# Batch normalisation of 32x256x128x128: the first tile's left half loaded in four pieces, the parameters in eight rows, 544 more columns for VectorE

## The chip, the cores and the metric

The kernel runs on one core of one Trainium2 chip. The metric is device time in microseconds (us). Before the change it is 2482.19 us, the median of three runs (2502.58, 2481.61 and 2482.19). One more execution was taken with the hardware profiler; every duration below comes from that one.

## The reference

```python
mean = running_mean.reshape(1, -1, 1, 1)
var = running_var.reshape(1, -1, 1, 1)
return gamma * (x - mean) / np.sqrt(var + 1e-5) + beta
```

All arrays are float32. `x` is 32x256x128x128 (536.9 MB) and so is the output; the four parameters have 256 values each. Per channel the computation is one multiply and one add, `x*scale + shift`, with `scale = gamma/sqrt(var + eps)` and `shift = beta - mean*scale`. Everything that is read is read once, and everything that is written is written once.

## The kernel before

**Tiles.** 256 channels are two blocks of 128, so `x` is cut into 64 tiles (`NT`) of 128 partitions x 16384 float32 (8.39 MB, 64 KB in each partition). Three buffers `bufs[0..2]` (`NBUF`) hold a tile each; a tile is loaded into a buffer, changed in place and stored from it.

**Loads.** SyncE (SP) issues all loads on its hardware queue. Tile 0 comes in two halves of 128x8192: the left half (line 89, semaphore `early`), then, behind the four parameter loads, the right half (line 96, semaphore `first[0]`). Tiles 1 and 2 follow whole (line 98). Tile i from 3 on (line 161) waits until the store of tile i-3 has freed its buffer (`stored`).

**Parameters.** Line 92 loads each of the four parameters as `NE` = 16 equal rows of 256 values (1 KB a row) into `rows`, a 32x1024 array that VectorE (DVE) has zeroed before (line 90; the first parameter load waits for that). When all four have landed (`fetched`), DVE transposes 32x32 blocks (line 109), copies four columns into place (line 113), and DVE and ScalarE (ACT) compute `scale_t` and `shift_t` (lines 115 to 125). The transpose reads row 0 of each block only, so one row would do for the values.

**Arithmetic.** Tile 0 is shared: DVE does columns 0 to 8191 as soon as the left half has landed (line 154, a wait for `early` at 16), then the columns up to `VHEAD` (line 155, after the right half); ACT does columns `VHEAD` to 16383. The last tile is shared in the same way at `VLAST` = 9216. All other tiles are ACT's alone (line 142 is the helper's activation, line 131 the helper's tensor_scalar).

**Stores.** GpSimd (POOL) issues the stores of tiles 0 to 60 through its software queue (line 173), each after ACT's part (`adone`), that of tile 0 also after DVE's two parts (`vdone`). ACT issues the last three itself. The order of work on every engine is written out by hand.

A DMA transfer's semaphore is raised by 16 in all when it has landed, so a wait at 16 is a wait for a whole transfer.

Of the kernel before, what the change touches and what calls it, by code (L numbers as in the profile page):

```python
# [9 lines left out]
PAD = 936  # L10
NHEAD = 3
NTAIL = 3
VHEAD = 8336
VLAST = 9216


@with_exitstack
def kernel(
# [9 lines left out]
    nc = tc.nc  # L28
# [4 lines left out]
    P = nc.NUM_PARTITIONS  # L33
    assert C % P == 0
    NCB = C // P
    HW = H * W
    NT = N * NCB
    B = 32
    NQ = P // B
    NE = 16  # L40
    NPAR = 4

    xr = x.rearrange("n (cb p) h w -> (n cb) p (h w)", p=P)
# [5 lines left out]
    bufs = [data.tile([P, HW], f32, name=f"t{s}", tag=f"t{s}") for s in range(NBUF)]  # L49
# [15 lines left out]
    early = tc.alloc_semaphore("early")  # L65
# [7 lines left out]
    with tc.tile_critical():  # L73
        count = [0]

        def step(inst, sem=None, value=None):
            if sem is not None:
                inst._wait_ge(sem, value)
            elif count[0]:
                inst._wait_ge(vec, count[0])  # L80
            inst.then_inc(vec, 1)
            count[0] += 1
            return count[0]

        left, right = slice(0, HW // 2), slice(HW // 2, HW)
        last = NT - 1


        nc.sync.dma_start(out=bufs[0][:, left], in_=xr[0][:, left]).then_inc(early, 16)
        zeroed = step(nc.vector.memset(rows[:], 0.0))  # L90
        for r, ap in enumerate((running_var, gamma, beta, running_mean)):
            inst = nc.sync.dma_start(out=rows[0:NE, r * C : (r + 1) * C], in_=ap.partition_broadcast(NE))  # L92
            if r == 0:
# [6 lines left out]
        def landed(i):  # L100
            if i < NHEAD:
                return first[i], 16
            s = i % NBUF
            before = 1 if s < NHEAD else 0
            return loaded[s], 16 * (i // NBUF + 1 - before)
# [6 lines left out]
        for q in range(NQ):  # L112
# [3 lines left out]
            out=std_t[:],  # L116
            in_=var_t,
# [11 lines left out]
        def vector_part(i, first_col, end):  # L129
            t, cb = bufs[i % NBUF], i % NCB  # L130
            return nc.vector.tensor_scalar(  # L131
                out=t[:, first_col:end],
                in0=t[:, first_col:end],
                scalar1=scale_t[:, cb : cb + 1],
                scalar2=shift_t[:, cb : cb + 1],
                op0=mybir.AluOpType.mult,
                op1=mybir.AluOpType.add,
            ).then_inc(vdone, 1)
# [12 lines left out]
        def share(i):  # L151
            return VHEAD if i == 0 else VLAST if i == last else 0

        vector_part(0, 0, HW // 2)._wait_ge(early, 16)
        vector_part(0, HW // 2, VHEAD)._wait_ge(first[0], 16)
        vector_part(last, 0, VLAST)._wait_ge(*landed(last))

# [57 lines left out]
```

## Time and profile before

| what | us |
|---|---|
| median of three runs | 2482.19 |
| profiled execution, its own time | 2482.56 |
| its span, first to last instruction | 2480.8 |
| first load issued (line 89) | 0.96 |
| left half landed, after its issue | 12.7 |
| right half landed, after its issue at 3.93 | 19.6 |
| first store issued (line 173) | 30.93 |
| last load landed, ACT starts the last tile | 2450.06 |
| last store issued by ACT | 2456.45 |

| engine | busy us | share of the span |
|---|---|---|
| DVE | 13.5 | 1% |
| ACT | 885.5 | 36% |
| POOL | 32.7 | 1% |

The profile's page gives the busy time of each engine, the share of the 16 DMA engines that were moving data in 40 equal slices of the span, the DMA queues (q1 is SP's hardware queue, q10 is ACT's, q0 is POOL's software queue) and the chain of waits that ended last. TensorE does nothing. The trace also holds each DMA packet with its start, duration, queue and size, and the time of each semaphore update by a DMA; it does not say which of the 16 engines carried a packet. A packet of a load or store is one partition's row.

### The profile page before, as it was taken

Reading aid. Unit: us, or ns where it says so; the run is one execution under the profiler, and the core shown is the slowest. Engines: PE = TensorE matmul, PEld = TensorE weight load, DVE = VectorE, ACT = ScalarE, POOL = GpSimd, SP = SyncE. Lnnn points to the kernel's source line nnn. Section 1 sums busy time; section 2 is a strip of 40 time slices with the busy share of each in tenths; the row PEclk is TensorE's granted clock in tenths of the full one; section 3 lists DMA queues with packets and bytes.
Section 4 is the critical chain, followed back from the end, with each engine's and each line's share of the span. In section 5 each row is a group of like instructions: output and inputs, shape, how many; then the busy total and the mean of one; then the engine's idle time right before and its main releaser. Section 6 shows DMA issues by size and latency. Waiting matters only on the chain.

```text
span 2480.8 us, 277 instructions
## 1 busy us (share of the span) xinstructions
DVE 13.5 (1%) x14; ACT 885.5 (36%) x66; POOL 32.7 (1%) x65
## 2 busy tenths in 40 slices
DVE  1000000000000000000000000000000000000000
ACT  2342433424324243242342423424334243342432
POOL 0000000000000000000000000000000000000000
DMA  9999999999999999999999999999999999999999
GB/s 413 433 431 431 440 435 427 440 439 424 440 439 424 440 439 424 440 439 428 435 439 431 432 440 434 428 440 435 427 440 437 425 440 439 424 440 439 426 437 406
DMA packets 18707, 1073.84 MB, mean 433 GB/s; under 512 B 2128, under 2 KB 2192, under 8 KB 2192
## 3 DMA queue, kind: packets, MB, share of 16 engines
q1 hardware_dynamic: 9488, 536.94, 50.0%
q0 software_dynamic: 8784, 511.71, 47.6%
q10 hardware_dynamic: 432, 25.17, 2.3%
q14 instruction: 3, 0.02, 0.0%
HBM read 536.94 MB, written 536.87 MB: 433 GB/s over the span
## 4 chain that ended last, share of the span: by engine, by line
another core or an unknown queue 61%; ACT 35%; DMA 2%; issue 0%; SPq 0%; DVE 0%; ACTq 0%; DVEq 0%
ACT t L142 35%; DMA t<-in_x_dram 2%; SPq L92 0%; DVE rows L90 0%; ACTq L173 0%; SPq L96 0%; DVE eps_t L108 0%; DVEq L210 0%; SPq L73 0%
## 5 line engine op out<-in xcount | busy, mean ns | idle before, releaser
L142 ACT ACTIVATE t<-t,shift_t,scale_t 128x16384 f32<-128x16384 f32 (+1 forms) x64 | 883.9, 13811 | 1555.8 <-DMA t<-in_x_dram 1555.8
L173 POOL DMA_DIRECT2D out_dram<-t x61 | 32.5, 533 | 2315.8 <-ACT t L142 2315.8
L131 DVE TENSOR_SCALAR t<-t,scale_t,shift_t 128x8192 f32<-128x8192 f32 (+2 forms) x3 | 10.0, 3326 | 2427.6 <-DMA t<-in_x_dram 2427.5
L115 ACT ACTIVATE std_t<-par,eps_t 128x2 f32<-128x2 f32 x1 | 0.3, 295 | 14.3 <-DVE par L113 14.3
L115 ACT ACT_TABLE_LOAD x1 | 1.3, 1283 | 0.9 <-SPq L73 0.9
L109 DVE STREAM_TRANSPOSE turned<-rows 32x1024 f32<-32x1024 f32 x1 | 1.2, 1232 | 12.1 <-DMA rows<-in_running_mean_dram 12.1
L90 DVE MEMSET rows<- 32x1024 f32 x1 | 0.9, 912 | 1.2 <-SPq L73 1.2
L113 DVE COPY par<-turned 32x8 f32<-32x8 f32 x4 | 0.6, 162 | 0.1
L122 DVE RECIPROCAL rstd_t<-std_t 128x2 f32<-128x2 f32 x1 | 0.2, 166 | 0.4 <-ACT std_t L115 0.4
L124 DVE TENSOR_TENSOR ms_t<-par,scale_t 128x2 f32<-128x2 f32 x1 | 0.2, 163 | 0.0
L123 DVE TENSOR_TENSOR scale_t<-par,rstd_t 128x2 f32<-128x2 f32 x1 | 0.2, 160 | 0.0
L125 DVE TENSOR_TENSOR shift_t<-par,ms_t 128x2 f32<-128x2 f32 x1 | 0.2, 160 | 0.0
L199 POOL MEMSET const-float32-0.0<- 128x1 f32 x1 | 0.1, 98 | 0.2 <-issue 0.2
L199 POOL MEMSET const-bfloat16-1.0<- 128x1 bf16 x1 | 0.1, 101 | 0.0
L199 POOL MEMSET const-float32-1.0<- 128x1 f32 x1 | 0.1, 98 | 0.0
L199 POOL MEMSET const-uint8-127<- 128x1 uint8 x1 | 0.1, 98 | 0.0
L108 DVE MEMSET eps_t<- 128x1 f32 x1 | 0.1, 59 | 0.1
## 6 DMA issues: line engine op xcount, KB each, us to landing
t<-in_x_dram SPq DMA_DIRECT2D x2, 4096.0 KB, 16.1
t<-in_x_dram SPq DMA_DIRECT2D x63, 56.0
out_dram<-t POOLq DMA_DIRECT2D x61, 45.5
out_dram<-t ACTq DMA_DIRECT2D x3, 32.0
rows<-in_running_var_dram SPq DMA_DIRECT2D x1, 16.0 KB, 11.2
rows<-in_gamma_dram SPq DMA_DIRECT2D x1, 16.0 KB, 11.1
rows<-in_beta_dram SPq DMA_DIRECT2D x1, 16.0 KB, 10.9
rows<-in_running_mean_dram SPq DMA_DIRECT2D x1, 16.0 KB, 10.9
```

The costliest lines, as they stand in the source:

```text
L90: zeroed = step(nc.vector.memset(rows[:], 0.0))
L109: step(nc.vector.transpose(out=turned[:], in_=rows[:]), fetched, 16 * NPAR)
L113: placed = step(nc.vector.tensor_copy(out=flat[q * B : (q + 1) * B], in_=blocks[:, :, q, 0]))
L115: nc.scalar.activation(out=std_t[:], in_=var_t, func=mybir.ActivationFunctionType.Sqrt, bias=eps_t[:], scale=1.0,)._wait_ge(vec, placed).t ...
L122: step(nc.vector.reciprocal(out=rstd_t[:], in_=std_t[:]), act, 1)
L123: step(nc.vector.tensor_mul(out=scale_t[:], in0=gamma_t, in1=rstd_t[:]))
L124: step(nc.vector.tensor_mul(out=ms_t[:], in0=mean_t, in1=scale_t[:]))
L125: ready = step(nc.vector.tensor_sub(out=shift_t[:], in0=beta_t, in1=ms_t[:]))
L131: return nc.vector.tensor_scalar(out=t[:, first_col:end], in0=t[:, first_col:end], scalar1=scale_t[:, cb : cb + 1], scalar2=shift_t[:, cb ...
L142: return nc.scalar.activation(out=t[:, first_col:], in_=t[:, first_col:], func=mybir.ActivationFunctionType.Identity, bias=shift_t[:, cb : ...
L173: eng.dma_start(out=outr[i], in_=bufs[i % NBUF][:], **packet)._wait_ge(adone, i + 1).then_inc(written, 16)
L199: nc = _bacc.Bacc("TRN2", target_bir_lowering=False, num_devices=1)
```

## The change

The left half of tile 0 is no longer one transfer of 128x8192 but four: columns 2304 to 8191 of all partitions, columns 0 to 2303 of partitions 16 to 127, and columns 0 to 2303 of partitions 0 to 7 and of partitions 8 to 15. All four raise `early`, and the first DVE part waits for 64 of it instead of 16. Each parameter is loaded in 8 equal rows instead of 16. `VHEAD` goes from 8336 to 8880, so DVE's second part of tile 0 has 688 columns instead of 144, and ACT's part 7504 instead of 8048.

```diff
-VHEAD = 8336
+VHEAD = 8880
+CUT = 2304
+ODD = 8
...
-    NE = 16
+    NE = 8
...
-        nc.sync.dma_start(out=bufs[0][:, left], in_=xr[0][:, left]).then_inc(early, 16)
+        side, most = slice(0, CUT), slice(CUT, HW // 2)
+        heads = [(slice(0, P), most), (slice(2 * ODD, P), side), (slice(0, ODD), side), (slice(ODD, 2 * ODD), side)]
+        for part, cols in heads:
+            nc.sync.dma_start(out=bufs[0][part, cols], in_=xr[0][part, cols]).then_inc(early, 16)
...
-        vector_part(0, 0, HW // 2)._wait_ge(early, 16)
+        vector_part(0, 0, HW // 2)._wait_ge(early, 16 * len(heads))
```

The order of instructions on DVE, ACT and POOL is the same as before; on SP three transfers are added ahead of the parameter loads.

## The prediction

> **What bounds the kernel.** I read the page first: span, digits of the DMA, queues.
>
> ```profile
> span 2480.8 us, 277 instructions
> ...
> DMA  9999999999999999999999999999999999999999
> ...
> HBM read 536.94 MB, written 536.87 MB: 433 GB/s over the span
> ```
>
> No slice has DMA below 90%, while ACT, the busiest engine, has 36%. So the 16 DMA engines are the bound; the question is whether their rate or their gaps can move. For that, busy times by stage, each row one tile period (the stores of consecutive tiles are issued 38.64 us apart) or a whole number of them; the columns are stretch, length, DVE, ACT, POOL, clock, DMA share, GB/s:
>
> ```profile
> 14.50:53.14 38.64, 7.32 (x11) 7.71 (x3) 0.67 (x1) 1.00 1.02 437
> 53.14:91.78 38.64, 0.00 (x0) 13.96 (x2) 0.53 (x1) 1.00 1.00 434
> 91.78:130.42 38.64, 0.00 (x0) 13.80 (x1) 0.53 (x1) 1.00 1.01 434
> 130.42:169.06 38.64, 0.00 (x0) 14.04 (x1) 0.53 (x1) 1.00 0.98 417
> 169.06:207.70 38.64, 0.00 (x0) 14.04 (x1) 0.53 (x1) 1.00 1.00 434
> ...
> 284.98:1057.78 772.80, 0.00 (x0) 280.79 (x20) 10.63 (x20) 1.00 1.00 434
> ```
>
> From 169 us on the rate stands at 434 GB/s, and 2 x 8.39 MB / 38.64 us is 434.2: 27.1 GB/s for each of the 16. In the packet records a 64 KB row takes 2418 ns, and the next begins 3 ns before its end, load or store alike. All 1073.84 MB at 434.2 GB/s are 2473.1 us. The span is 7.7 us more: **nothing at the head can gain more than 7.7 us, 0.3%**. From the packet records the 7.7 are: 1.97 until the first packet; 0.6 more for the first packets, which take 1.81 us on average and not 1.21; 0.2 for their spread (they start from 1.97 to 2.82, mean 2.18); 0.6 around the parameter packets (an engine's last left packet ends at 12.50 on average, its first right packet at 14.32: 1.82 for a packet of 1.21); 1.5 of packets lengthened while the stores join (19 packets by 9.0 us together at 31 to 36 us, 27 by 4.5 at 91 to 101, 25 by 8.6 at 129 to 138, hardly any after; 23.9 in all over 16 engines); 0.8 by which the slowest engine ends (2478.65) after the mean of all (2477.86); 2.15 from there to the end. That is 7.8.
>
> Now the head, in order of time (start, duration, engine, line):
>
> ```profile
> 0.96 0.37 SPq L89 DMA_DIRECT2D t<-in_x_dram  x1
> ...
> 2.16 0.34 SPq L92 DMA_DIRECT2D rows<-in_running_var_dram  x1
> ...
> 3.93 0.44 SPq L96 DMA_DIRECT2D t<-in_x_dram  x1
> 4.41 1.02 SPq L98 DMA_DIRECT2D t<-in_x_dram  x2
> 14.40 1.23 DVE L109 STREAM_TRANSPOSE turned<-rows 32x1024 f32<-32x1024 f32 x1 [12.14 <-DMA rows<-in_running_mean_dram]
> ...
> 17.64 4.55 DVE L131 TENSOR_SCALAR t<-t,scale_t,shift_t 128x8192 f32<-128x8192 f32 x1
> 23.53 7.09 ACT L142 ACTIVATE t<-t,shift_t,scale_t 128x8048 f32<-128x8048 f32 x1 [6.79 <-DMA t<-in_x_dram]
> 23.53 0.35 DVE L131 TENSOR_SCALAR t<-t,scale_t,shift_t 128x144 f32<-128x144 f32 x1 [1.34 <-DMA t<-in_x_dram]
> 30.93 0.67 POOL L173 DMA_DIRECT2D out_dram<-t  x1 [30.49 <-ACT t L142]
> ```
>
> The reader is to see that everything is issued by 5.43 us while the left half keeps the engines until 12.3: issue has 7 us of cover.
>
> **The change, part by part.**
>
> *SP.* Three more issues of 0.37 to 0.5 us put the last head piece at about 2.6 us. The first parameter load, which waited until 2.16 for the memset, goes at about 2.65; it, the right half and tiles 1 and 2 move back by 0.5 us. Behind 7 us of cover that costs nothing; without cover, the 0.5.
>
> *Left half.* The bytes are the same, the division over engines may not be. In the queue rows of the page the parameter loads show one packet a row (2192 packets under 2 KB less 2128 under 512 B are 64, which is 4 loads of 16 rows), so an eight-row transfer has eight packets and touches eight engines at most; the trace has no such transfer and cannot say which. The 112 rows are seven for each of 16. If both eight-row pieces go to the same eight engines, these get nine rows of 9216 B and the others seven; one row is 9216 B / 27.1 GB/s = 0.34 us, so +0.34 for eight engines and -0.34 for eight. If they go to different eights, zero. The packets of 9216 B that replace part of the 32 KB ones cost between nothing (64 KB and 32 KB packets run at the same rate) and a parameter packet's bubble (0.6 us for four, 0.15 each) for the two odd rows.
>
> *Parameters.* Eight rows are eight packets: at least eight engines lose a transfer's packet, and the 0.6 us around four of them falls to zero there if it is always the same eight; the other eight keep it.
>
> *Sum.* The kernel ends when its slowest engine does. The last store's sixteen updates come at 2477.79 to 2478.37 us and one at 2479.00. With everything on the same eight, the loaded engines shift by +0.34 and the others by -0.34 - 0.6 = -0.94. If the straggler is among the relieved, the end is 2478.37 + 0.34 = 2478.71 at most, -0.3 us; if among the loaded, +0.34; with 0.3 for the two odd packets, +0.6. The trace does not say which; that engine's lag is mostly its lengthened packets (2.1 us, the others 1.2 to 1.6), and those come after the head. The mean over all engines is (0.34 - 0.94)/2 = -0.3, and the bounds' middle is about +0.1. I take **-0.2**, nearer the mean, as the loaded engines' lag is the only thing pushed up.
>
> The Trainium skill (DMA: Bandwidth & Descriptors, section on why a DMA increments its semaphore by 16 and not by 1) says that a transfer uses the largest number of engines up to 16 that divides its outermost dimension, on a hardware queue the lowest-numbered ones. By that all six eight-row transfers fall on the same eight, and the sum is the first case; no row here shows it.
>
> *DVE, ACT.* 544 columns cost DVE 544 x 4.55/8192 = 0.30 us, hidden under ACT's part, which falls by 544 x (7.09 - 6.36)/(8048 - 7168) = 0.45 to 6.64 (6.36 is ACT's row on the last tile's 7168 columns). The first store goes at about 30.5 to 30.9, as the right half may land up to 0.35 later. Parameters up to 0.35 later make DVE's left part end at 22.6, still before 23.5. An earlier store gains nothing: the engines have loads of tiles 1 and 2 to move until 91 us, and total bytes decide.
>
> **The numbers.** The profiled execution took 2482.56, its span and 1.76 around it; the sum gives 2482.36, and the median of the three runs is 0.37 below the profiled one: **2482.0**.
>
> **Rivals.**
>
> 1. *Start-up contention goes* (12%). The two eights would run 1.28 us apart (0.34 + 0.94), half of a 2418 ns packet, when the stores join. Lengthened packets die out once engines are spread, which speaks for it; against, the spread before was already 0.6 us and did not help. Price: a third to all of 1.5 us, 2480.7 to 2481.5.
>
> 2. *The pieces cost a fixed time each, or contention at the head grows* (14%). With one more round of lengthened packets (0.6 us, that of 31 to 36 us) up to double the 1.5, 2482.6 to 2483.5 and above. Against a fixed cost: four parameter loads between two halves cost 0.6 us together. The Trainium skill (DMA: Bandwidth & Descriptors, anatomy of one DMA) fits 2.0 us plus bytes/436 GB/s to one transfer and advises against small ones. By that three more transfers in a row would add 6 us, 2488; four parameter loads in 0.6 us disagree, as the queue overlaps them.
>
> 3. *Contention that does not die out* (8%), the slower side. The shift of phases at the stores' joining could leave a pattern in which packets are lengthened in every tile. Place: the first packets of each load, as at 129 to 138 us. Price: that round's 8.6/16 = 0.54 us x 60 tiles = 32 us, 2514; it exceeds 1% from 0.41 us a tile. For it: the run of 2502.58 is 20 us over the others, 0.33 us a tile, and no profile explains it. Against: every period from 169 us on is at 434.
>
> 4. *The split does nothing* (3%): the odd rows spread evenly, 2482.2.
>
> My forecast, 2481.6 to 2482.7, has the remaining 63%.
>
> **Range and chances.** 2480.6 to 2484.2: rival 1 below; above, +0.6 and double contention (+1.5). It leaves out rival 3 and half of rival 2, 15%. A measurement of this kernel can tell about 1%, 25 us, from no change. Faster by that is excluded by the 7.7 us (1% is kept for what I overlook); slower needs half of rival 3, 4%; within 1%: 95%.
>
> **What would show it.** Right: periods from 169 us on at 434 GB/s; 32 packets between 512 B and 2 KB in place of 64; the left half landing over a spread 0.7 us wider than before; transpose at 14.4 to 14.8; ACT's first part about 6.64; first store near 30.7. Wrong: a period below 430 after 200 us (rival 3); a DMA gap at 2 to 12 us (rival 2); periods up to 169 us all at 434 and an end below 2481.5 (rival 1).

## The result and the profile after

The changed kernel takes 2509.24 us (median of 22 runs, 2494.13 to 2517.89), the kernel before, on the same chips, 2493.71 us (22 runs, 2481.52 to 2509.59). The ratio is 1.0057, 95% interval 1.0034 to 1.0079: slower by 0.6%, and outside the range that was forecast. The kernel before is not one number: of 149 runs beside all kernels of this study 68 lie under 2486 us, the rest between 2486 and 2523. Of the changed kernel's 22 runs none is under 2494.

The page of the profiled execution after (its own time 2508.31 us): span, share of the DMA engines and GB/s in 40 slices.

```profile
span 2506.5 us, 280 instructions
...
DMA  9999999999999999999999999999999999999997
GB/s 402 435 434 433 435 427 431 430 434 435 435 431 434 431 435 435 432 433 434 433 434 424 431 429 426 430 429 435 430 434 429 426 429 429 432 434 426 428 430 345
DMA packets 18803, 1073.81 MB, mean 428 GB/s; under 512 B 2128, under 2 KB 2160, under 8 KB 2160
```

The engines are still counted as busy in every slice but the last, and yet they move 428 GB/s and not 433. Busy times by stage, after (columns as before: stretch, length, DVE, ACT, POOL, clock, DMA share, GB/s):

```profile
14.50:53.14 38.64, 7.71 (x11) 6.93 (x2) 0.67 (x1) 1.00 1.00 428
53.14:91.78 38.64, 0.00 (x0) 14.04 (x1) 0.53 (x1) 1.00 1.00 434
...
284.98:671.38 386.40, 0.00 (x0) 140.40 (x10) 5.32 (x10) 1.00 1.00 433
...
1057.78:1444.18 386.40, 0.00 (x0) 140.39 (x10) 5.32 (x10) 1.00 1.00 431
1444.18:1830.58 386.40, 0.00 (x0) 140.40 (x10) 5.31 (x10) 1.00 1.00 430
...
2216.98:2448.82 231.84, 0.00 (x0) 80.16 (x6) 2.12 (x4) 1.00 1.00 429
```

Before, this column was 434 from 169 us to the end (one period at 436); the two last rows of before:

```profile
1057.78:1830.58 772.80, 0.00 (x0) 280.79 (x20) 10.63 (x20) 1.00 1.00 434
1830.58:2448.82 618.24, 0.00 (x0) 224.63 (x16) 7.44 (x14) 1.00 1.00 434
```

After, it is 434 early and falls to 429: the loss is spread over the run and grows. The head and the tail, in order of time:

```profile
16.88 1.23 DVE L114 STREAM_TRANSPOSE turned<-rows 32x1024 f32<-32x1024 f32 x1 [14.62 <-DMA rows<-in_running_mean_dram]
...
25.86 6.64 ACT L147 ACTIVATE t<-t,shift_t,scale_t 128x7504 f32<-128x7504 f32 x1 [6.63 <-DMA t<-in_x_dram]
...
32.80 0.67 POOL L178 DMA_DIRECT2D out_dram<-t  x1 [32.36 <-ACT t L147]
...
2475.72 6.36 ACT L147 ACTIVATE t<-t,shift_t,scale_t 128x7168 f32<-128x7168 f32 x1 [22.82 <-DMA t<-in_x_dram]
...
2482.11 0.34 ACTq L178 DMA_DIRECT2D out_dram<-t  x1
```

The right half lands 2.3 us later than before (ACT starts at 25.86, before 23.53). And in the tail something new: stages of the tail, after and then before.

```profile
2474.00:2483.00 9.00, 5.08 (x1) 6.36 (x1) 0.00 (x0) 1.00 0.35 153
```

```profile
2448.50:2457.50 9.00, 5.08 (x1) 6.36 (x1) 0.00 (x0) 1.00 1.04 451
```

While the last tile is computed, the engines used to be busy with the store before it; now they are busy for 35% of the time. The reason shows in the semaphore updates of the DMA: the sixteen parts of the last load landed within 1.2 us of each other before (2448.8 to 2450.0) and within 22.5 us after (2453.2 to 2475.7), so most engines had nothing left to move when the last part came.

**Where 25.7 us of span went**, from the packet records, as means over 16 engines: 2.1 us at the head (the engines' last packet of the right half ends at 24.9 on average, before 22.8); 16.7 us of 64 KB packets that take longer than 2418 ns, where before had 1.5; 7.5 us of idle engines, nearly all between 2472 and 2483 us. 2.1 + 15.2 + 7.5 = 24.8, and the engines' mean end moved from 2477.9 to 2502.6, by 24.7. The time by which packets are lengthened, per engine and tile period, in the kernel after: 0.17 us up to 140 us, 0.10 up to 700, 0.15 up to 1200, 0.35 up to 1800, 0.39 to the end. Before had next to none after 140 us (0.6 us over all engines together).

### The profile page after: what moved, and what is told of

It reads as the page before. It is cut to its first block, busy times and chain, and to the rows that moved or that the text cites. A ratio compares the mean times of both kernels' runs of the same rounds, so it can differ in the third digit from the quotient of the medians.

```text
span 2506.5 us, 280 instructions
## 1 busy us (share of the span) xinstructions
DVE 13.8 (1%) x14; ACT 885.0 (35%) x66; POOL 32.7 (1%) x65
## 2 busy tenths in 40 slices
DMA packets 18803, 1073.81 MB, mean 428 GB/s; under 512 B 2128, under 2 KB 2160, under 8 KB 2160
## 4 chain that ended last, share of the span: by engine, by line
another core or an unknown queue 63%; ACT 35%; DMA 1%; SPq 0%; issue 0%; ACTq 0%
ACT t L147 35%; DMA t<-in_x_dram 1%; SPq L94 0%; SPq L97 0%; ACTq L178 0%; SPq L215 0%; SPq L75 0%
## 5 line engine op out<-in xcount | busy, mean ns | idle before, releaser
L120 ACT ACTIVATE std_t<-par,eps_t 128x2 f32<-128x2 f32 x1 | 0.3, 296 | 16.7 <-DVE par L118 16.7
```

Of the source, the lines that this page charges most:

```text
L120: nc.scalar.activation(out=std_t[:], in_=var_t, func=mybir.ActivationFunctionType.Sqrt, bias=eps_t[:], scale=1.0,)._wait_ge(vec, placed).t ...
```

## The experiments

In each, "free" is a run under 2486 us. The five profiles of such runs (2482.08 to 2483.04 us) show at most 0.6 us of lengthened packets an engine after 140 us, and all profiles from 2496 us up show 13 us or more. The first theory was that the uneven division over engines puts two eights of them apart inside a packet, so that loads and stores never fall into step. One part of the change at a time, and the pieces without the uneven division:

**Only VectorE's share.**

```diff
-VHEAD = 8336
+VHEAD = 8880
```

> VHEAD 8880 alone, everything else as before. The theory (uneven division: the two groups of eight DMA engines reach the first store some 0.8 us apart, and the packets never fall into the lockstep in which eight load while eight store): this kernel has no uneven division, so it behaves as before, some runs at 2481 to 2485 and the others up to 2510, ratio within 0.997 to 1.003. Rival A (the time at which the first store joins decides, and ACT's shorter part moves it): no run under 2490, median about 2505. Rival B (the slow small packets of the head decide): as before.

Measured: median 2507.96, 1 of 12 runs free, ratio 1.0069 (1.0034 to 1.0104). The theory had this as harmless; it is enough by itself, near to what rival A had (median about 2505), though two runs lie under its 2490. The first store was issued at 30.45 us; the five profiles of the kernel before have 30.69 to 30.94.

**Only the parameters.**

```diff
-    NE = 16
+    NE = 8
```

> Parameters in eight rows alone. The theory: half of the unevenness (the 0.6 us around the parameter packets fall to eight engines alone), so fewer runs at 2481 to 2485 than before or none, median 2495 to 2510; the right half lands in two groups some 0.5 us apart. Rival A and rival B: as before, with some runs at 2481 to 2485.

Measured: median 2495.65, 5 of 12 free, ratio 1.0031 (0.9992 to 1.0071): not told from before. ACT started at 23.23; five profiles of the kernel before have 23.29 to 23.53, so fewer parameter packets save little at the head. The two groups that the theory expected at the right half do not show: its parts land from 22.6 to 23.2 us without a gap.

**Only the pieces** (the `heads` of the change, its wait for 64, `NE` 16, `VHEAD` 8336).

> The left half in four pieces alone, parameters in sixteen rows, VHEAD 8336. The theory: uneven by 0.68 us, no run under 2490, median 2500 to 2512. Rival A: as before, with some runs at 2481 to 2485. Rival B: no run under 2490, median 2500 to 2512. ACT starts the first tile at 25 to 26 us instead of 23.5 whatever the theory.

Measured: median 2511.33, 0 of 10 free, ratio 1.0091 (1.0061 to 1.0121); ACT started at 26.02. The theory and rival B both had this, so the run does not part them.

**Two even pieces.**

```diff
-        heads = [(slice(0, P), most), (slice(2 * ODD, P), side), (slice(0, ODD), side), (slice(ODD, 2 * ODD), side)]
+        heads = [(slice(0, P), most), (slice(0, P), side)]
```

> The left half in two pieces of all 128 partitions (5888 and 2304 columns), parameters in sixteen rows, VHEAD 8336: small packets, but no uneven division. The theory: as before, with some runs at 2482 to 2487 (up to 2 us later for the head), ratio 0.998 to 1.003. Rival B (small packets at the head): no run under 2490, median 2500 to 2512. Rival A: as before or a little later.

Measured: median 2482.82, 9 of 12 free, ratio 0.9981 (0.9950 to 1.0012); ACT started at 23.74. A piece of 9216 B a row costs 0.2 us when it has all 128 rows.

What falling into step looks like can be read from the packet records of the profile before: from 300 us on, eight loads and eight stores are under way through most of a tile's period.

The sixteen semaphore updates of a transfer tell what `VHEAD` does. When the load of tile 1 lands, the engines come in groups: those that took a packet of the first store at one packet boundary, and those that took it at the next. I worked out the groups at tiles 1 and 2 of each profile (the count in the earlier and the later group, and the step in us between the two groups' medians; 16/0 is a single group):

```
kernel                       tile 1            tile 2          lengthened per engine
                                                               after 140 us, us
before                       8/8,  2.2 us      8/8,  2.2 us     0.0
after                        8/8,  3.2         8/8,  3.2       16.1
VHEAD 8880                   16/0              16/0            20.4
NE 8                         8/8,  2.4         8/8,  2.4       22.1
pieces only                  8/8,  3.0         8/8,  3.0       20.4
two even pieces              10/6, 2.2         10/6, 2.0        0.1
VHEAD 9798                   16/0              15/1, 1.9       26.4
VHEAD 11260                  9/7,  2.2         16/0            26.8
VHEAD 11010                  14/2, 2.5         15/1, 1.3       13.7
uneven by a whole packet     5/3/6/2, 2.0-2.9  5/3/6/2, 2.1-2.8  20.9
sixteen-row piece            13/3, 2.9         13/3, 2.9       16.5
cut of 576                   4/12, 2.4         4/12, 2.1        0.6
share in every tile          8/8,  2.1         8/8,  2.2       13.5
after, share in every tile   8/8,  3.2         8/8,  3.2       14.2
before, further profiles     7/9,  2.3         7/9,  2.3       13.4
                             10/6, 2.1         10/6, 2.1        0.1
                             5/11, 2.1         5/11, 2.1       18.6
                             7/9,  2.1         7/9,  2.1       14.0
two even pieces, again       11/5, 2.3         11/5, 2.3        0.1
VHEAD 8208                   7/9,  2.2         7/9,  2.2       13.3
```

With `VHEAD` 8880 all sixteen take the store at the same boundary (16/0). So the second theory: the first store must split the engines into two groups, one packet apart. It makes a forecast for a change of `VHEAD` alone, by half a packet and by a whole one.

```diff
-VHEAD = 8336
+VHEAD = 9798
```

> Before with VHEAD 9798: ACT's part of tile 0 is 1462 columns shorter, so the first store is issued some 1.2 us earlier, half of a 64 KB packet's 2.415 us. The theory (the run settles only if the engines are split in two by the first store, half of them taking a store packet at one packet boundary and half at the next, with all boundaries aligned): the store becomes visible between two rounds of boundaries, all 16 engines take it at the same one, no split; nearly all runs over 2490, median 2500 to 2512. Rival (an earlier store is worse in proportion): about as bad as VHEAD 8880 or worse, 2508 and more.

Measured: median 2511.59, 0 of 12 free, ratio 1.0064 (1.0033 to 1.0095); all sixteen join together, as the theory had it. The time itself lies in the forecast of the theory and in that of the rival. Its stages:

```profile
130.42:169.06 38.64, 0.00 (x0) 14.04 (x1) 0.53 (x1) 1.00 1.00 434
284.98:1057.78 772.80, 0.00 (x0) 280.79 (x20) 10.63 (x20) 1.00 1.00 430
...
1830.58:2448.82 618.24, 0.00 (x0) 213.41 (x17) 7.97 (x15) 1.00 1.00 429
```

The same fall from 434 to 429 as in the kernel after, and earlier, with nothing changed but the division of tile 0 between DVE and ACT, and with it the moment of the first store.

**VHEAD 11260**, a whole packet.

> Before with VHEAD 11260: the first store is issued 2.415 us earlier, a whole packet. The theory: the store meets the same phase of the boundaries as before, one round earlier, and splits the engines as before; half or more of the runs at 2481 to 2486, median 2482 to 2496. Rival (an earlier store is worse): no run under 2490, median over 2505.

Measured: median 2507.18, 0 of 12 free, ratio 1.0054 (1.0023 to 1.0085). The theory's forecast fails; the rival's holds but for its lowest run, 2487.00. The split came as forecast at tile 1 (9/7), and was gone at tile 2 (16/0): the first store now ended some 2.4 us earlier on the first engines (its first part landed at 69.3 us, before 71.7), but the second store's packets started no earlier (73.9 us, before 73.8), so all sixteen engines took two loads in a row, at 69 and at 71.4 to 72.2 us, and joined anew, together. That reading was made after the run.

**VHEAD 11010.**

> Before with VHEAD 11010: a whole packet less 0.2 us earlier, which is the phase that the kernel with two even pieces had (its first store is issued 0.2 us later than before's, and 9 of its 12 runs were under 2486). The theory: like that kernel, two thirds or more of the runs at 2481 to 2486. Rival (an earlier store is worse): no run under 2490.

Measured: median 2508.02, 1 of 12 free, ratio 1.0061 (1.0023 to 1.0100). 14/2 at tile 1, 15/1 at tile 2. The theory's forecast fails again. The rival's is met but for one run of 2483.93: an earlier first store was bad at all four values, though not in proportion to how much earlier it came.

**Uneven by a whole packet.**

```diff
+CUT = 8192
...
+        heads = [(slice(2 * ODD, P), side), (slice(0, ODD), side), (slice(ODD, 2 * ODD), side)]
```

> Before with the whole left half divided unevenly: partitions 16 to 127 and twice eight rows, all 8192 columns, so eight engines have nine rows of 32 KB and eight have seven: the two eights are apart by two such rows, 2.42 us, a whole 64 KB packet, in place of 0.55 to 0.85 us. The theory (it is the offset within a packet that prevents lockstep): settles again, a third or more of the runs at 2481 to 2488. Rival (any uneven division is bad, through its unequal load or its small transfers): no run under 2490, median 2505 to 2515.

Measured: median 2508.74, 0 of 12 free, ratio 1.0073 (1.0033 to 1.0113). Inconclusive: ACT started at 35.18 us, so the head was not the one that was meant (see the last section), and the engines came in four groups of 5, 3, 6 and 2.

**The sixteen-row piece**, the pieces without the uneven division.

```diff
-        heads = [..., (slice(0, ODD), side), (slice(ODD, 2 * ODD), side)]
+        heads = [..., (slice(0, 2 * ODD), side)]
```

> The four-piece head with its two eight-row pieces joined into one of sixteen rows (parameters in sixteen rows, VHEAD 8336), so that the rows divide evenly over 16 engines, and the same columns and the same 112-row piece stay. Theory (uneven division puts the two eights 0.5 us apart inside a packet, so lockstep is never reached): settles as the kernel with two even pieces does, a third or more of 12 runs under 2486, median 2481 to 2497. Rival (small pieces and the 112-row transfer as such): no run under 2490, median 2505 to 2515.

Measured: median 2511.73, 0 of 12 free, ratio 1.0065 (1.0029 to 1.0101). The first theory falls as the only cause: the division is even and no run is free. Its rival, the 112-row transfer as such, fits the median; the lowest run is 2489.03. The split is 13/3 with a step of 2.9 us, so the second theory is not touched.

**A cut of 576 columns.**

> The four-piece head with a cut of 576 columns in place of 2304 (parameters in sixteen rows, VHEAD 8336): the same four transfers, a quarter of the offset (0.13 to 0.17 us, less than the 0.6 us by which engines are spread anyway). Theory: settles in a third or more of 12 runs (under 2486). Rival (eight-row transfers as such): no run under 2490.

Measured: median 2498.51, 1 of 12 free, ratio 1.0019 (0.9981 to 1.0057): fewer free runs than expected, at a ratio that is not told from before. The profiled run was the free one, with 4/12.

**VectorE's share in every tile**, before and after (`VALL`, 8192 columns of each tile by DVE; each store also waits for DVE).

```diff
+VALL = 8192
...
-            return VHEAD if i == 0 else VLAST if i == last else 0
+            return VHEAD if i == 0 else VLAST if i == last else VALL
...
-        vector_part(last, 0, VLAST)._wait_ge(*landed(last))
+        for i in range(1, NT):
+            vector_part(i, 0, share(i))._wait_ge(*landed(i))
...
-            if i in (0, last):
-                eng.wait_ge(vdone, 2 if i == 0 else 3)
+            eng.wait_ge(vdone, i + 2)
```

> Before, with VectorE doing 8192 columns of every tile as it does of the first, so every store is issued some 7 us earlier. Theory as above (the phase at which the packets meet decides, and it is drawn at the first store): about as often settled as before, 3 to 7 of 12 runs under 2486, the others 2490 to 2505 (less than before's, if no engine's store queue runs dry). Rival (the lag grows because ACT's 14 us make late stores later, so store queues run dry): 11 or 12 of 12 runs under 2486.

> The changed kernel, with VectorE doing 8192 columns of every tile. Theory: still no run under 2486, since the two eights are apart by 0.85 us inside a packet; median 2492 to 2512. Rival (late stores): most runs under 2488.

Measured: before with shares 2488.70, 5 of 12 free, ratio 0.9987 (0.9954 to 1.0020); after with shares 2502.31 (2492.73 to 2511.02), 0 of 12 free, ratio 1.0035 (1.0005 to 1.0065). (A sixth run of before with shares, at 2486.15, is just over the line.) Stores that are issued 7 us earlier free no run of the kernel after and no more runs of the one before, so late stores are not what decides. The runs that are not free reach 2501 with shares in the kernel before, and 2518 without on the same chip, which suggests that late stores add to the loss once engines lag; that was not tested further.

**The kernel before, four more profiles.** Does the split decide within one program?

> The kernel before, unchanged, for one more profile; the same for the three others. Theory (the split of the 16 engines at the first store decides, also between runs of one program): where the time is under 2486, the second tile's load lands in two groups of at least four engines, one packet apart (1.9 to 2.7 us), and no packet is lengthened after 140 us; where it is over 2490, the groups are 13/3 or more unequal, or off by over 0.5 us from one packet. Rival (the split follows the program alone and something else decides): 8/8 within 2.0 to 2.5 us in slow and fast runs alike.

The three others had the same expectation in short. Measured: 2497.33, 2482.73, 2510.64 and 2500.09 us. The second theory's strong form falls: 7/9, 5/11 and 7/9 with steps of 2.1 to 2.3 us are in the runs that are not free, 10/6 with 2.1 in the free one. The stages of the first and the second of them:

```profile
130.42:169.06 38.64, 0.00 (x0) 14.03 (x2) 0.53 (x1) 1.00 1.01 434
169.06:207.70 38.64, 0.00 (x0) 14.04 (x1) 0.53 (x1) 1.00 0.99 426
284.98:1057.78 772.80, 0.00 (x0) 280.79 (x20) 10.63 (x20) 1.00 1.00 432
```

```profile
130.42:169.06 38.64, 0.00 (x0) 14.01 (x2) 0.53 (x1) 1.00 1.00 434
169.06:207.70 38.64, 0.00 (x0) 13.96 (x2) 0.53 (x1) 1.00 1.00 434
284.98:1057.78 772.80, 0.00 (x0) 280.81 (x21) 10.63 (x20) 1.00 1.00 434
```

One program, one chip, and from 285 to 2449 us the rate is 431 to 432 in the one run and 434 in the other.

**Two last runs**: the best kernel again, and a first store 0.1 us later.

```diff
-VHEAD = 8336
+VHEAD = 8208
```

> The kernel with the left half in two pieces of all 128 partitions once more, on whatever chip comes, since 9 of its 12 runs were under 2486 and this is the only kernel that may beat the one before. If that is the program's: 7 or more of 12 runs under 2486, median 2482 to 2484, ratio under 1. If it was chance or that chip: about as many as before (4 to 6 of 12, as of all runs of before so far), median 2482 to 2497, ratio 0.998 to 1.002.

> Before with VHEAD 8208, so ACT's part is 128 columns longer and the first store is issued 0.1 us later. If it is the moment of the first store against the packet boundaries that decides (0.48 us earlier left 1 of 12 runs under 2486; 0.2 us later, with two even pieces, 9 of 12): at least as many as before, 6 or more of 12. If 0.1 us does not matter: 4 to 6 of 12, ratio 0.998 to 1.002. If any change of the head loses it: 0 to 2 of 12.

Measured: two even pieces 2492.00, 5 of 12 free, ratio 1.0008 (0.9961 to 1.0055); `VHEAD` 8208 2494.63, 5 of 12 free, ratio 1.0007 (0.9966 to 1.0049). The 9 of 12 were luck in part: 14 of 24 in all, against 68 of 149 for before. No kernel of this study is shown to beat the one before.

**What the runs show together.** Of 8 profiles in which at tile 2 fewer than four engines are in one of the groups, or the groups are more than half a microsecond off one packet, none is free, and their eight kernels have 2 free runs of 104. Of 11 profiles with two groups of at least four engines about a packet apart, 5 are free. The one with four groups (uneven by a whole packet) is not. The lines between these kinds were drawn when 14 of the 20 profiles had been seen. So a split in step looks necessary, and is not sufficient. That the moment of the first store can lose it, with the loads of the head as they were, is shown by `VHEAD` (2 free runs of 48 at 8880, 9798, 11010 and 11260). In the kernel after itself the first store comes later than before, not earlier (32.80 against 30.93), since the pieces delay it by more than `VHEAD` saves; there the step of 3.2 us is off a packet by about the 0.8 us by which the two eights are apart in the right half. Open are what lengthens a packet at all, and what else picks the free runs among those in step; no kernel changed the addresses or the order of rows, and each kernel has one profile, so the split of its other runs was not seen.

## Why the prediction was wrong

**The bound was right.** The DMA engines were and are the bound, and the time follows from their packets.

**The step that failed** is the end of the part on DVE and ACT: "An earlier store gains nothing", because "total bytes decide", and with it the sum, which let the head act on the end only through bytes per engine. When the first store comes, and where each engine then stands in its packets, was put at nothing. The lengthened packets stood in it as a start-up cost of 1.5 us that dies out. In the kernel after they do not: 16.7 us an engine, and then 7.5 us idle in the tail, because engines that lag by 20 us hold back the last tile. That was rival 3, and its sign, a period below 430 after 200 us, came (429). That its price (32 us, 2514) is near the measured 27 us over the before profile's 2482 is partly luck: it had 0.54 us in every tile, the trace has 0.10 to 0.39, and the head and the idle tail, which it did not have, add 2.1 and 7.5. It got 8%, on the ground that every period of the one profile from 169 us on was at 434. A period that is constant in one run says how that run went, not that the next run goes so: one of the three times was 2502.58, and the text itself worked out that it was 0.33 us a tile. Its mechanism, a shift of phases when the stores join, is near what the runs show; but the shift need not come from the two eights, since `VHEAD` alone does it and the even sixteen-row piece does it too. Its place, the first packets of each load, was wrong for about half: 7.8 of the 16.1 us an engine after 140 us are in stores. What lengthens a packet stays open.

**The base was wrong too.** 2482.19 was the median of three; of 149 runs fewer than half are near it.

**The left half.** Its small packets were priced between nothing and 0.3 us, its odd rows at 0.34. It cost 2.1 to 2.3. The packets of 9216 B took 531 ns on average, not 340: about 0.19 us x 7 to 9 packets, an estimate of 1.3 to 1.7 us; the rest is around the first packets of the right half. The odd rows were suspected and the 112-row piece was not. The two eights were forecast 1.28 us apart (0.68 by the rows, 0.6 by the parameters); the right half's parts land in two eights 0.8 us apart, 0.6 with the pieces alone. The fit of the Trainium skill that rival 2 quotes (DMA: Bandwidth & Descriptors, anatomy of one DMA) is given there for the software queue, while these loads go on SP's hardware queue; one more transfer cost 0.2 us in the two even pieces.

**Right in its parts.** Issue: the first parameter load at 2.57 (2.65 forecast) and the right half at 3.98, hardly later than before, so nothing was lost to it. ACT's part 6.64, DVE's second part 0.64. 32 packets between 512 B and 2 KB (2160 less 2128). The eight-row transfers use eight engines each: the head's semaphore has 50 updates that the trace puts down to DMA, of which two come at 2.3 and 2.7 us, 7 us ahead of the first data, and 48 with data, 16 + 16 + 8 + 8. That they are the same eight fits the two eights in which the right half lands, where before has one group. The Trainium skill (DMA: Bandwidth & Descriptors, section on why a DMA increments its semaphore by 16 and not by 1) says that a transfer on k engines gets k updates from them and the other 16 - k at once from the issuing sequencer; the trace agrees with the counts and the times, and does not name the engines. **Wrong in time**: the transpose at 16.88 (14.4 to 14.8), the first store at 32.80 (near 30.7), both behind the slow pieces.

## What to carry to other kernels

When a kernel keeps all DMA engines busy with loads and stores, an edit of 0.5 us at its start can choose how packets meet for the rest of the run. Price it by the spread between runs of the same program, not by the bytes it moves. Take many runs before calling one profile the kernel, and look at a single outlier of three as a second way in which the program runs. In such a profile the sixteen landing times of each transfer say more than the busy share, which stays at 9 tenths while packets are lengthened.

## What the hardware did that was not expected

**A transfer of 112 partitions can be slow by the byte.** Packets of 9216 B took 347 ns (median) in the 128-row piece of the kernel with two even pieces, and 513 to 533 ns (medians of three kernels) in the 112-row and shorter pieces. In the kernel that is uneven by a whole packet, packets of 32 KB took 2.06 us while the 112-row transfer ran, and 1.21 us in the right half. The cut of 576 columns does not show it: its 112-row and eight-row pieces have packets of 2304 B of 93 ns (median), where 27.1 GB/s gives 85, so the number of rows alone does not explain it. The Trainium skill (DMA: Bandwidth & Descriptors, section on the descriptor swizzle) describes how in a 128-partition transfer each engine writes the partitions of one SBUF port; that 7 rows an engine break this and engines meet at ports is my reading, no run here shows ports, and the cut of 576 speaks against it as the whole cause.

**The software queue's first store starts late.** From POOL's issue to the first store packet it took 4.2 us before (30.93 to 35.11) and 4.4 after (32.80 to 37.20), and 3.9 to 5.4 in all twenty profiles: nearly two packets, in which a packet boundary may or may not fall.

**Lengthening has its place.** Here a tile's period is counted from ACT's start on the tile. In two of the further profiles of before (2497.33 and 2500.09 us), loads are lengthened at 0.50 to 0.65 of the period, around the time when parts of a store land. The profile before passes the same place, with all sixteen engines loading at once, with none. In the profiles that drift most, stores are lengthened at 0.40 to 0.45 of the period (18 us of 26.4 an engine with `VHEAD` 9798).
